# Chunk states in three rounded products, and three changes of order, in a two-layer decoder trunk

## The chip, the cores and the metric

The kernel runs on one core of a Trainium2 chip. A core has a matrix engine (TensorE, PE in the profile; its weight loads are shown apart as PEld), a vector engine (VectorE, DVE), a scalar engine for activations and copies (ScalarE, ACT), a general engine (GpSimd, POOL) and queues that issue transfers (SyncE, SP, and those of the other engines). They run side by side, each through its own list of instructions in order, and wait for each other on semaphores. SBUF is the memory that the engines work in, PSUM holds what PE writes, in banks of 512 numbers a partition.

The metric is the time of one execution on the device in microseconds (us), as the median of several runs.

## What is computed

The reference is a decoder trunk of two layers over 1040 tokens (16 learned ones and 1024 of input) of width 1024, in float32. Layer 0 is a state space mixer, layer 1 attention, and each is followed by a feed forward network (FFN) with a causal convolution.

```python
# mixer, by chunk of tokens
cb = einsum('bclgn,bcsgn->bgcls', c_c, b_c)
y_diag = einsum('bgcls,bgecls,bcsgep->bclgep', cb, decay_in, xdt)
chunk_states = einsum('bclgn,bgecl,bclgep->cbgepn', b_c, decay_to_end, xdt)
state = state * d + s_new            # over the chunks, in order
y_off = einsum('bclgn,cbgepn,bgecl->bclgep', c_c, prev_states, exp(a_cs))
# attention, stick-breaking
logits = einsum('bthd,bshd->bhts', q, k) * scale
log_keep = where(visible, log_sigmoid(-logits), 0)
w = exp(where(visible, log_sigmoid(logits) + later, -inf))
o = einsum('bhts,bshd->bthd', w, v)
# FFN
h = causal_conv(u @ w_up);  g, val = split(h);  (silu(g) * val) @ w_down
```

The mixer has 4 groups of 8 heads, a state of 128 by 64 for each head; attention has 16 heads of width 64.

## The kernel before

**Rounded parts.** A float32 number x is split in a high part, x rounded to the matrix engine's faster format (float32r), and a low part, x less the high one. A product of two such numbers is then made of three products, high by high, high by low and low by high, added in one PSUM bank (`mm3`, lines 209 to 211). Nearly all large products are made so. A high part is a copy on ACT, a low part a subtraction on DVE or POOL.

**The mixer** (`mixer`, `ssd_decays`, `ssd_front`, `ssd_back`). The 1040 tokens lie in nine chunks of 116 (the last has 112). For each of the four groups it runs through the nine chunks; between them it runs pieces of the projections of the next groups (`next(work)`: 24 matmuls with an ACT filter tap and three DVE taps behind them), as many to a chunk as SHARES says: two in groups 0 and, mostly, 3, three or four in groups 1 and 2. In a chunk, `ssd_front` transposes B (`bk`) and x, makes `cbm`, `xdt` (x times dt, on DVE) and `xde` (xdt times the decay to the chunk's end, on POOL in two pieces, behind the pieces of `E` that are made there for the same chunk); then come the projection pieces; then `ssd_back` makes the chunk's state `S` from `bk` and `xde` in one float32 product (line 799), adds it to the running state, and makes the outputs `y`. Eight of the nine chunks of a group have an S: 32 products. The whole loop is written out by hand: PE, DVE, ACT and POOL keep the order of the program (`manual_schedule`).

**Attention** (`attention`, `heads`). Eight pairs of heads, each in 18 steps (i, jj): token block i of 116, key tile jj of 348 tokens, jj from i // 3 down to 0. Steps 0 to 2 have one key tile each, steps 3 to 8 are blocks 3 to 5 with tiles 1 and 0, steps 9 to 17 are blocks 6 to 8 with tiles 2, 1 and 0. A step starts with `weigh`: the logits `lg` on PE (line 1653), two sigmoids on ACT (1654, 1655), two scans and a product `bt` on DVE (1664, 1665). Then come the halves of the projections that fall due (table `halves`, 12 matmuls each), what the step before left in `late`, a chore (rounding the next weights), and `flush`, which transposes the weights of two steps before (`turn`, wT, line 1687) and, when a visit of blocks is done, multiplies the values (`values`, po, line 1710). These four engines keep the program's order here too.

The table `halves` gives the keys so: tile 2 of a pair's own keys at its steps 4 and 5, tiles 0 and 1 of the next pair's keys at steps 8, 9 and 14, 15. For the last pair, tile 2 comes at steps 0 and 1. After the second half DVE multiplies the product by the norm factor (`t`, line 1577); one step later `key` splits `t`: a copy on ACT (line 1588, the high part), a subtraction on DVE (`klo`, line 1589), and three transfers on SP's queue (lines 1590 to 1592) that put the high and low parts of the two heads above each other in the two key tiles. The logits of a head read both halves of its tile. Tile 2 is first read in step 9.

The first half of the output projection runs as units beside the last pair (`o_blocks`): a unit is 12 matmuls into a bank (`accumulate`) and a DVE addition of that bank to `h` (line 538). In the loop of the last pair each step from 5 on runs one unit; after it (`while turns or ready`) two units run ahead of each remaining turn, the first two of them in the two halves of the tile that the logits used.

**FFN, up projection** (`enter_ffn`, `forms`, `up`). The product with w_up is made by a fast scheme of seven half-size products, `product(0)` to `product(6)` of a block, with sums and differences of quarters of the input (`forms`: t1, t2, t3 ... and their rounded parts) and of the weights. The input's second half of tokens is t = 1. A block adds the first sum (`add(y, y, p1)`), and then the third product's sum, `add(z, z, u2)`, line 1237 by its helper, to which product 5 adds. For the first block, `forms` of t = 1 is a generator that advances one `yield` with every part of the block: in its steps it multiplies `h` by the norm's factors (`product(K, ...)` and `product(range(KD // 2, KD), ...)`, eight DVE instructions, line 1091), makes t1 and t2 (line 1115), and rounds the forms (lines 1097, 1098). Here the framework's planner orders the engines by simulated times and the order of the program; `behind` adds a wish for an order that costs no semaphore.

Of the kernel before, what the change touches and what calls it, by code (L numbers as in the profile page):

```python
# [105 lines left out]
class Trunk:  # L106
    def __init__(self, ctx, tc, a):
        self.tc, self.nc, self.a = tc, tc.nc, a
        nc = self.nc
        self.cp = ctx.enter_context(tc.tile_pool(name="cp", bufs=1))  # L110
        self.qp = ctx.enter_context(tc.tile_pool(name="qp", bufs=NQ))
        self.tmps = ctx.enter_context(tc.tile_pool(name="up", bufs=8))
        self.wp = ctx.enter_context(tc.tile_pool(name="wp", bufs=3))
        self.mp = ctx.enter_context(tc.tile_pool(name="mp", bufs=2, space=bass.MemoryType.PSUM))
        self.sp = ctx.enter_context(tc.tile_pool(name="sp", bufs=SMB, space=bass.MemoryType.PSUM))
        self.dp = ctx.enter_context(tc.tile_pool(name="dp", bufs=1, space=bass.MemoryType.DRAM))
        self.lp = None
        self.n = 0
        self.open = []
        self.hold = self.copy_tie = self.silu_tie = None  # L120
        self.consts()
# [406 lines left out]
    def accumulate(self, h, f, s0, n, w, ks, front=0, bank=None, base=0, new=False):  # L528

        ps = (bank or (self.ex if f % 3 == 2 else self.mm))("acc")  # L530
        c, o = slice(s0 - base, s0 - base + n), slice(front + s0, front + s0 + n)
        for i, (hi, lo) in enumerate(ks):
            wh, wl = w(i, f)
            self.mm3(ps[:, :n], wh, wl, hi[:, c], lo[:, c], i == 0, i == len(ks) - 1)
        if new:
            self.nc.vector.tensor_copy(h[f][:, o], ps[:, :n])
        else:
            self.nc.vector.tensor_tensor(h[f][:, o], h[f][:, o], ps[:, :n], op=ALU.add)
# [220 lines left out]
    def ssd_front(self, g, x, bt, ct, c, dk, pool):  # L759
# [16 lines left out]
        if c < 8:  # L776
            bk = pool.tile([P, P], F32, tag="bk", name=self.nm("bk"), bufs=2)
            nc.scalar.activation(bk[:n], pcb[:n, P : 2 * P], AF.Copy)
        cbm = pool.tile([P, CB], F32, tag="cbm", name=self.nm("cbm"), bufs=2)
# [4 lines left out]
        if c < 8:  # L784
            xde = pool.tile([P, GH, 64], F32, tag="xde", name=self.nm("xde"), bufs=2)
            pieces(nc.gpsimd, xde[:n], xdt[:n], self.cols[:n, 2, cc, h0 : h0 + GH].unsqueeze(2).to_broadcast([n, GH, 64]), ALU.mult)
        return xdt, xde, bk

    def ssd_back(self, g, x, c, dk, ce, xdt, xde, bk, states, pool):
# [7 lines left out]
        if c < 8:  # L797
            ps = self.lg("S")
            nc.tensor.matmul(ps, bk[:n], xde[:n].rearrange("p h d -> p (h d)"), start=True, stop=True)  # L799
# [23 lines left out]
    def mixer(self, mx):  # L823
# [12 lines left out]
        with self.tc.tile_pool(name="ssd", bufs=3) as pool:  # L836
# [27 lines left out]
            with self.tc.manual_schedule(engines={E.PE, E.DVE, E.Activation, E.Pool}):  # L864
                ahead = self.ssd_decays(0, rows[0][5], 0, pool)
                dk, ce = next(ahead)
                for g in range(GROUPS):
# [3 lines left out]
                    for c in range(9):  # L871
# [8 lines left out]
                        for _ in range(sum(share[: c + 1]) - given):  # L880
                            next(work)
                            if not begun:
                                begun = True
                                nxt = (g, ct, c + 1) if c < 8 else (g + 1, rows[g + 1][5], 0) if g < 3 else None
                                ahead = self.ssd_decays(*nxt, pool) if nxt else iter([(None, None)])
# [189 lines left out]
    def forms(self, layer, h, r, t, tiles, pool):  # L1075
# [11 lines left out]

        def product(ks, part):
            c = slice(new.start, s.start + N) if part == 0 else slice(s.start + N, new.stop)
            for k in ks:  # L1090
                nc.vector.scalar_tensor_tensor(h[k][:, c], h[k][:, c], self.par(gain, k), r[:, c], op0=ALU.mult, op1=ALU.mult)

# [26 lines left out]
        if t:  # L1119
            product(range(KD // 2, KD), 0)  # L1120
            yield
            product(K, 1)
            yield
            t1 = minus(b12, b11)
            product(range(KD // 2, KD), 1)
            yield
            t2 = minus(b22, t1)
# [73 lines left out]
    def up(self, layer, w0, forms, rest, pool):  # L1201
# [8 lines left out]
        def block(b, t, w, late=None):  # L1210
# [35 lines left out]
            p5 = copy(z)  # L1246
            add(z, z, u2)
            yield
# [266 lines left out]
    def heads(self, u, p, pool):  # L1515
# [4 lines left out]
        class Pair:  # L1520
# [38 lines left out]
            def half(me, kind, j, h, bank=None, parts=2):  # L1559
# [16 lines left out]
                if kind == "k":  # L1576
                    nc.vector.tensor_tensor(t[:, :n], ps[:, :n], u[KD][:, o:e], op=ALU.mult)
                    return [lambda: me.key(j, t)]
                nc.scalar.activation(t[:, :n], ps[:, :n], AF.Copy)
# [139 lines left out]
    def attention(self, u, pool, hd):  # L1719
# [34 lines left out]
        for kind, j, bank in (("k", 0, self.mm), ("q", 0, self.mm), ("k", 1, self.sm), ("q", 1, self.ex)):  # L1754
            for h in range(2):
                for f in first.half(kind, j, h, bank):
                    f()
            if (kind, j) == ("k", 0):
                self.late_factors()
        self.token_factors(u[KD], pool)  # L1760
        for p in range(PAIRS):
            prev = None
            for n, (i, jj) in enumerate(steps):
# [14 lines left out]
                for own, pair in now.items():  # L1778
                    if p + 1 < PAIRS and (own, n) in halves:
                        late += pair.half(*halves[own, n])  # L1780
                for f in todo + chores[:1]:
                    f()
# [7 lines left out]
        banks = iter([lambda s, a=a: both[:, a] for a in range(2)])  # L1790
        self.unit_bank = lambda s: next(banks, self.mm)(s)
        while turns or ready:
            next(behind)
            next(behind)
            flush(0)
        return od, behind
# [261 lines left out]
```

## Time and profile before

| what | before |
|---|---|
| median of 3 runs | 2857.06 us (2851.83 to 2860.83) |
| profiled execution, its own time | 2855.13 us |
| its span, first to last instruction | 2853.3 us |
| granted PE clock, mean | 0.997 |
| ACT, POOL busy | 55%, 55% |
| mixer's chunk loop | about 115 to 600 us |
| attention's steps | about 1538 to 2067 us |
| the up projections' starts | about 830 to 860 and 2157 to 2183 us |

Busy time of an engine is the time in which it ran an instruction; it says nothing of whether that work was on the path that set the end. A row of a group reads: line, engine, operation, what it wrote and read, shapes, count, busy time. A row of the timeline gives start and duration in us, and in brackets the idle time before it with what ended it. "PE x <- DVE y" means that PE stood still until DVE had written y. The granted clock is the share of full speed that the matrix engine was given.

### The profile page before, as it was taken

How to read it: one execution, taken by the hardware profiler on the slowest of the kernel's cores; microseconds unless marked ns; L12 is line 12 of the kernel's file. 1: busy time of each engine (PE TensorE's matmuls, PEld its weight loads, DVE VectorE, ACT ScalarE, POOL GpSimd, SP SyncE). 2: the span in 40 equal slices, each digit the busy share in tenths (PEclk: the TensorE clock that was granted, in tenths of full speed). 3: DMA queues.
4: the chain of work that ended last, by engine and by line, in shares of the span. 5: the costliest groups of instructions: out<-in, count | busy, mean ns of one | idle time of the engine just before them, and what ended most of it. 6: DMA issues, size and time to landing. Idle time of an engine off the chain costs nothing.

```text
span 2853.3 us, 56464 instructions
## 1 busy us (share of the span) xinstructions
PE 2809.2 (98%) x21251; PEld 2691.9 (94%) x21251; DVE 2065.4 (72%) x3936; ACT 1580.2 (55%) x3077; POOL 1578.6 (55%) x2144
## 2 busy tenths in 40 slices
PE   8999999999999999999999999999999999999998
PEld 7989999999999999999999999999899999999888
DVE  5676666668487676767886888888749676766776
ACT  5554554543256555555335777777536555555433
POOL 2366455553519888867763212112254888886881
PEclk9999999999999999999999999999999999999999
DMA  4333333343413222235142222222532222225331
GB/s 119 86 112 93 121 83 125 116 136 101 120 64 96 78 80 78 79 135 176 49 142 77 74 73 69 80 70 57 184 131 77 82 80 82 75 82 185 111 104 67
DMA packets 141740, 281.78 MB, mean 99 GB/s; under 512 B 16307, under 2 KB 71740, under 8 KB 141468
## 3 DMA queue, kind: packets, MB, share of 16 engines
q1 hardware_dynamic: 135844, 267.01, 29.8%
q0 software_dynamic: 2048, 6.49, 0.6%
q10 hardware_dynamic: 3576, 4.67, 0.5%
q8 instruction: 168, 2.75, 0.4%
q14 instruction: 104, 0.85, 0.1%
HBM read 207.79 MB, written 55.42 MB: 92 GB/s over the span
## 4 chain that ended last, share of the span: by engine, by line
PE 91%; DVE 4%; ACT 2%; POOL 1%; issue 1%; DMA 0%; SPq 0%; ACTq 0%; DVEq 0%; POOLq 0%
PE p L209 10%; PE p L210 10%; PE p L211 10%; PE acc L209 8%; PE acc L211 8%; PE acc L210 8%; PE pj L209 8%; PE pj L210 8%; PE pj L211 8%; PE po L1710 3%; PE lg L1653 2%; PE wT L1687 2%; PE y L810 1%; PE S L799 1%; PE y L812 1%; PE ms L1069 1%
## 5 line engine op out<-in xcount | busy, mean ns | idle before, releaser
L102 POOL TENSOR_TENSOR wl<-w,wh 128x256 fp32r<-128x256 f32 x760 | 678.9, 923 | 352.2 <-ACT wh L196 225.4
L209 PE MATMUL pj<-uh,wh 128*128 128x348 f32 (+2 forms) x1536 | 500.4, 326 | 2.1 <-DVE xbc L339 1.4
L210 PE MATMUL pj<-ul,wh 128*128 128x348 f32 (+2 forms) x1536 | 494.9, 322 | 0.8 <-DVE ul L320 0.8
L211 PE MATMUL pj<-uh,wl 128*128 128x348 f32 (+2 forms) x1536 | 492.0, 320 | 0.0
L209 PE MATMUL p<-bh,fh 128*128 128x262 f32 (+1 forms) x1408 | 400.9, 285 | 3.9 <-DVE p L1237 3.7
L211 PE MATMUL p<-bh,fl 128*128 128x262 f32 (+1 forms) x1408 | 401.0, 285 | 0.9 <-POOL fl L102 0.9
L210 PE MATMUL p<-bl,fh 128*128 128x262 f32 (+1 forms) x1408 | 399.2, 284 | 0.0
L102 POOL TENSOR_TENSOR fl<-x,fh 128x256 fp32r<-128x256 f32 x352 | 264.3, 783 | 186.8 <-ACT fh L1174 160.9
L210 PE MATMUL p<-bl,wh 128*128 128x262 f32 (+1 forms) x1040 | 295.6, 284 | 1.1 <-DVE bl L1098 1.1
L209 PE MATMUL p<-bh,wh 128*128 128x262 f32 (+1 forms) x1040 | 295.3, 284 | 0.4 <-ACT ft L1234 0.4
L211 PE MATMUL p<-bh,wl 128*128 128x262 f32 (+1 forms) x1040 | 294.1, 283 | 0.0
L209 PEld LDWEIGHTS pj<-uh,wh 128*128 128x128 f32 x1536 | 288.7, 188 | 4.5 <-ACT xbc L336 1.7
L210 PEld LDWEIGHTS pj<-ul,wh 128*128 128x128 f32 x1536 | 289.2, 188 | 2.4 <-DVE ul L320 1.4
L211 PEld LDWEIGHTS pj<-uh,wl 128*128 128x128 f32 x1536 | 288.7, 188 | 0.1
L339 DVE SCALAR_TENSOR_TENSOR c<-p,params,c 128x260 f32<-128x260 f32 (+1 forms) x528 | 248.4, 480 | 54.7 <-ACT c L336 48.3
L209 PEld LDWEIGHTS p<-bh,fh 128*128 128x128 f32 x1408 | 268.0, 191 | 4.7 <-DVE p L1237 4.1
L211 PEld LDWEIGHTS p<-bh,fl 128*128 128x128 f32 x1408 | 267.1, 190 | 1.6 <-POOL fl L102 1.5
L210 PEld LDWEIGHTS p<-bl,fh 128*128 128x128 f32 x1408 | 267.8, 190 | 0.5 <-DVE bl L1098 0.4
L1234 ACT ACTIVATE ft<-p 128x262 f32<-128x262 f32 (+1 forms) x352 | 133.2, 382 | 179.9 <-DVE p L1237 110.1
L210 PE MATMUL acc<-gl,wh 128*128 128x260 f32 (+1 forms) x672 | 214.2, 320 | 0.0
L211 PE MATMUL acc<-gh,wl 128*128 128x260 f32 (+1 forms) x672 | 213.2, 319 | 0.0
L209 PE MATMUL acc<-gh,wh 128*128 128x260 f32 (+1 forms) x672 | 210.8, 320 | 0.1
(336 smaller groups left out, 7690.6 us busy)
## 6 DMA issues: line engine op xcount, KB each, us to landing
w<-in_w_up SPq DMA_DIRECT2D x88, 512.0 KB
w<-in_w_down SPq DMA_DIRECT2D x44, 512.0 KB
w<-in_w_in SPq DMA_DIRECT2D x40, 512.0 KB
E<-ea_d SPq DMA_DIRECT2D x32, 464.0 KB
D<-acs_d SPq DMA_DIRECT2D x32, 420.5 KB
g<-c SPq DMA_DIRECT2D x88, 130.0 KB
g<-c SPq DMA_DIRECT2D x88, 128.0 KB
b<-g SPq DMA_DIRECT2D x16, 520.0 KB
```

The costliest lines, as they stand in the source:

```text
L102: done.append(eng.tensor_tensor(out[:, c], x[:, c], y[:, c], op=op))
L209: self.behind(mm(out, wh, uh, start=first, stop=False, skip_group_check=joins), tie, "behind the sums of squares")
L210: mm(out, wh, ul, start=False, stop=False, skip_group_check=joins)
L211: self.last_mm = mm(out, wl, uh, start=False, stop=last, skip_group_check=joins)
L339: ins = nc.vector.scalar_tensor_tensor(out, ps[:, o + i : o + i + n], wcol(i), out, op0=ALU.mult, op1=ALU.add)
L799: nc.tensor.matmul(ps, bk[:n], xde[:n].rearrange("p h d -> p (h d)"), start=True, stop=True)
L810: nc.tensor.matmul(y, xdt[:n, i, :], dk[:, i, :], start=True, stop=c == 0)
L812: nc.tensor.matmul(y, state[:, i, :], ce[:, i, :], start=False, stop=True)
L1234: nc.scalar.activation(s[:, :N], ps[:, :N], AF.Copy)
L1653: nc.tensor.matmul(ps[:nt, a, :m], part[:, c0 : c0 + nt], ks[a][:, s0 : s0 + m], start=x == 0, stop=x == 1)
L1687: nc.tensor.transpose(pt[:ns, x * CB : x * CB + nt], bt[:nt, a, x * CB : x * CB + ns], self.ident[:nt, :nt])
L1710: nc.tensor.matmul(po[64 * a : 64 * a + 64, t0:n], v[: CH[c][1], c, 64 * a : 64 * a + 64], wt[a][q][: CH[c][1], r, t0:n], start=x == 0, st ...
```

## The change

There are four edits.

1. The chunk states: `bk` is kept as high and low part (ACT copy, DVE subtraction from PSUM), `xde` is split in high and low part by the new `split_xde` (ACT copy, DVE subtraction), called after the first projection piece of a chunk, and S is made by `mm3`. The tiles `bk`, `xdh`, `xdl` and `xde` have one buffer each.
2. In attention, what a key's second half leaves for the next step is now a function that leaves `key` for the step after that. The first pair's own keys, made ahead of the loop, are split as before.
3. For the first pass of the loop after the last pair, the additions of the two units are collected and run after both units have multiplied.
4. In `forms` for t = 1, the second half of the second factor products moves one `yield` later, in front of t1, and each of them is ordered behind the third sum.

```diff
         if new:
             self.nc.vector.tensor_copy(h[f][:, o], ps[:, :n])
+        elif self.adds is not None:
+            self.adds.append(lambda: self.nc.vector.tensor_tensor(h[f][:, o], h[f][:, o], ps[:, :n], op=ALU.add))
...
-            bk = pool.tile([P, P], F32, tag="bk", name=self.nm("bk"), bufs=2)
-            nc.scalar.activation(bk[:n], pcb[:n, P : 2 * P], AF.Copy)
+            bk = pool.tile([P, 2, P], F32R, tag="bk", name=self.nm("bk"), bufs=1)
+            nc.scalar.activation(bk[:n, 0], pcb[:n, P : 2 * P], AF.Copy)
+            tt(bk[:n, 1], pcb[:n, P : 2 * P], bk[:n, 0].bitcast(F32), op=ALU.subtract)
...
-            xde = pool.tile([P, GH, 64], F32, tag="xde", name=self.nm("xde"), bufs=2)
-            pieces(nc.gpsimd, xde[:n], xdt[:n], self.cols[:n, 2, cc, h0 : h0 + GH].unsqueeze(2).to_broadcast([n, GH, 64]), ALU.mult)
+            xde = [pool.tile([P, GH, 64], dt, tag=t, name=self.nm(t), bufs=1) for t, dt in (("xdh", F32R), ("xdl", F32R), ("xde", F32))]
+            pieces(nc.gpsimd, xde[2][:n], xdt[:n], self.cols[:n, 2, cc, h0 : h0 + GH].unsqueeze(2).to_broadcast([n, GH, 64]), ALU.mult)
         return xdt, xde, bk
+
+    def split_xde(self, xde, c):
+
+        if xde:
+            hi, lo, t = (t[: CH[c][1]] for t in xde)
+            self.nc.scalar.activation(hi, t, AF.Copy)
+            self.nc.vector.tensor_tensor(lo, t, hi.bitcast(F32), op=ALU.subtract)
...
-            nc.tensor.matmul(ps, bk[:n], xde[:n].rearrange("p h d -> p (h d)"), start=True, stop=True)
+            hi, lo = (t[:n].rearrange("p h d -> p (h d)") for t in xde[:2])
+            self.mm3(ps, bk[:n, 0], bk[:n, 1], hi, lo, True, True)
...
                             if not begun:
                                 begun = True
+                                self.split_xde(ops[1], c)
...
-        def product(ks, part):
+        def product(ks, part, tie=None):
...
-                nc.vector.scalar_tensor_tensor(h[k][:, c], h[k][:, c], self.par(gain, k), r[:, c], op0=ALU.mult, op1=ALU.mult)
+                ins = nc.vector.scalar_tensor_tensor(h[k][:, c], h[k][:, c], self.par(gain, k), r[:, c], op0=ALU.mult, op1=ALU.mult)
+                self.behind(ins, tie, "behind the third sum")
...
             product(K, 1)
             yield
+            yield
+            product(range(KD // 2, KD), 1, self.third_sum)
             t1 = minus(b12, b11)
-            product(range(KD // 2, KD), 1)
-            yield
             t2 = minus(b22, t1)
...
-            add(z, z, u2)
+            self.third_sum = add(z, z, u2)
...
-                    return [lambda: me.key(j, t)]
+                    return [lambda: [lambda: me.key(j, t)]]
...
-                for f in todo + chores[:1]:
+                for f in todo:
+                    late += f() or []
+                for f in chores[:1]:
                     f()
...
+        self.adds = []
         while turns or ready:
             next(behind)
             next(behind)
+            for f in self.adds or ():
+                f()
+            self.adds = None
             flush(0)
```

More of the change, by code (lines that the diff above doesn't have):

```diff
@@ L119, in __init__ @@
         self.open = []
-        self.hold = self.copy_tie = self.silu_tie = None
+        self.adds = self.hold = self.copy_tie = self.silu_tie = None
         self.consts()
@@ L1756, in attention @@
                 for f in first.half(kind, j, h, bank):
-                    f()
+                    for g in f() or ():
+                        g()
             if (kind, j) == ("k", 0):
```

## The prediction

> **What bounds the kernel now.** I read the page from the top: busy times, then the chain that ended last, then the waits of the matrix engine (PE).
>
> ```profile
> span 2853.3 us, 56464 instructions
> PE 2809.2 (98%) x21251; PEld 2691.9 (94%) x21251; DVE 2065.4 (72%) x3936; ACT 1580.2 (55%) x3077; POOL 1578.6 (55%) x2144
> PE 91%; DVE 4%; ACT 2%; POOL 1%; issue 1%; DMA 0%; SPq 0%; ACTq 0%; DVEq 0%; POOLq 0%
> ```
>
> PE is busy 98% of the span and makes 91% of the chain. Only two things can move the time: PE work, and PE waits. The profiled execution took 2855.13 us (its span and 1.8 around it), 1.9 below the median of 2857.06; the sums below stand on 2855.13. The waits that this change can touch, in us in total, times, longest:
>
> ```profile
> PE lg L1653 <- ACT bt L1655: 6.3, 11, 0.8
> PE acc L209 <- DVE h L538: 4.3, 2, 3.3
> PE p L209 <- DVE p L1237: 3.7, 2, 1.9
> PE S L799 <- POOL xde L102: 1.4, 3, 0.6
> ```
>
> Each edit has one of these rows or makes one longer. A wait has a second price, seen in stretches of the trace (busy time of PE, PEld, DVE, ACT and POOL; the last three numbers are the granted clock, the DMA share and GB/s):
>
> ```profile
> 844.95:848.35 3.40, 3.40 (x17) 3.40 (x17) 3.40 (x12) 2.97 (x9) 0.00 (x0) 0.50 0.00 0
> 2060.10:2066.90 6.80, 5.87 (x30) 4.74 (x32) 1.30 (x4) 0.00 (x0) 0.00 (x0) 0.50 0.91 329
> 2169.30:2172.70 3.40, 3.01 (x25) 3.02 (x26) 3.40 (x11) 2.71 (x9) 0.00 (x0) 1.00 0.00 0
> ```
>
> After a PE gap of 1.86 us at 841.8 the clock was 0.50 for 3.4 us; after one of 3.31 at 2057.7 it was 0.50 for 6.8; after the other wait of p (3.7 less 1.86, 1.8 us, at 2167.9) it stayed at 1.00. Half clock costs half its length: 1.7, 3.4 and 0 us.
>
> **Chunk states.** 32 products S leave their single form for three rounded ones. First the PE work:
>
> ```profile
> 229.22 0.86 PE S L799 x2
> 1636.69 0.32 PE L210 MATMUL pj<-ul,wh 128*128 128x348 f32 x1
> 1638.29 0.33 PE L211 MATMUL pj<-uh,wl 128*128 128x348 f32 x1
> ```
>
> One S is two records and 0.86 us on the chain. Rounded products of 348 columns start 0.16 apart (ten steps from 1636.69 to 1638.29). The trace has no rounded product of 512 columns: in proportion it is 0.235, three are 0.71 (between 0.48, were the pitch fixed, and 0.86, no gain). I take 0.71, the proportional one: 0.15 x 32 = 5 us less PE work.
>
> Then the new links. S waited for xde (POOL); now it waits for xde, a copy on ACT and a subtraction on DVE. The first two pairs of rows are chunks of groups 3 and 0, the third is of group 1, and the last two rows are the nearest copy and (two pieces) subtractions of this size:
>
> ```profile
> 571.83 1.46 POOL L102 TENSOR_TENSOR xde<-xdt,cols 116x256 f32<-116x256 f32 x2
> 573.34 1.12 PE L799 MATMUL S<-xde,bk 116*128 116x512 f32 x2
> 155.71 1.18 POOL L102 TENSOR_TENSOR xde<-xdt,cols 116x256 f32<-116x256 f32 x2
> 157.42 1.02 PE L799 MATMUL S<-xde,bk 116*128 116x512 f32 x2
> 158.29 1.80 DVE L339 SCALAR_TENSOR_TENSOR xbc<-pj,params,xbc 128x344 f32<-128x344 f32 x3 [2.02 <-ACT xbc L336]
> 235.92 1.18 POOL L102 TENSOR_TENSOR xde<-xdt,cols 116x256 f32<-116x256 f32 x2
> 243.03 0.59 PE L799 MATMUL S<-xde,bk 116*128 116x512 f32 x1
> 855.31 0.62 ACT L1174 ACTIVATE wh<-w 128x512 fp32r<-128x512 f32 x1
> 856.58 1.29 DVE L1178 TENSOR_TENSOR wl<-w,wh 128x512 fp32r<-128x512 f32 x2
> ```
>
> The split takes 0.62 + 0.65 and about 0.05 for each of three hand-overs: 1.4 us. In groups 1 and 2 S starts 6 us after xde: hidden. In groups 0 and 3, 13 chunks have 0.05 (573.29 to 573.34) to 0.9 us. At 157.42 the slack is 0.53, so S would stand 0.9. The chunk behind gets part of that back, because its POOL work starts from DVE work that the late S does not hold (DVE was idle 2.02 us before 158.29, which also hides the extra subtraction of bk, while ACT holds only a tap behind xde). Without that return the 13 waits come to 12, with half of it returned to some 7 to 9; I take 9.5, since the two first chunks, with 0.05, hold their own filters back too. Sum: 9.5 - 5 = **+4.5** (from -10, hidden and at the fixed pitch, to +8).
>
> **Keys a step later.** What it removes: the key's copy stands in ACT's queue between one step's sigmoids and the next and waits for DVE.
>
> ```profile
> 1642.29 0.49 ACT L1588 ACTIVATE k<-k 128x348 fp32r<-128x348 f32 x1 [0.79 <-DVE k L1577]
> 1646.15 0.68 PE L1653 MATMUL lg<-k,qs 128*116 128x232 f32 x4 [0.65 <-ACT bt L1655]
> ```
>
> That is step 11 of pair 1; pairs 0 to 6 show it, seven of the eleven waits, 0.65 each: -4.5. One step later the product that it copies is done, and ACT no longer stands still for it.
>
> What it adds: every key tile moves, also the third of a pair's own keys. Its halves run at steps 4 and 5, its split moved from step 6 to 7, and step 9 is the first whose logits read those columns. Pair 1:
>
> ```profile
> 1630.70 0.88 DVE L1665 TENSOR_TENSOR bt<-bt,kp 116x696 f32<-116x696 f32 x1
> 1631.50 0.51 DVE L1589 TENSOR_TENSOR klo<-k,k 128x344 fp32r<-128x344 f32 x1
> 1633.67 1.64 DVE L1664 TENSOR_TENSOR_SCAN kp<-kp,one 116x349 f32<-116x349 f32 x2
> 1635.42 0.88 DVE L1665 TENSOR_TENSOR bt<-bt,kp 116x696 f32<-116x696 f32 x1
> 1632.62 0.55 SPq L1592 DMA_DIRECT2D k<-klo  x1
> 1633.10:1634.40 1.30, 1.30 (x10) 1.30 (x9) 1.30 (x3) 1.18 (x3) 0.00 (x0) 1.00 0.61 136
> 1635.74 0.60 PE L1653 MATMUL lg<-k,qs 128*116 128x116 f32 x4
> 1700.76 0.88 DVE L1665 TENSOR_TENSOR bt<-bt,kp 116x696 f32<-116x696 f32 x1
> 1700.72 0.49 PE L1653 MATMUL lg<-k,qs 128*116 128x116 f32 x3
> ```
>
> The subtraction (klo) stands behind bt of step 6 and ends at 1632.01. Its two transfers are issued by 1633.17, and the stretch to 1634.40 moves 136 GB/s x 1.3 = 177 KB, both of them (86 KB each): landed 2.39 us after klo's end, 1.3 ahead of the logits of step 9. DVE works without a pause here and is behind PE: bt of step 7 ends at 1636.30, when PE already stands at step 9. The moved klo goes behind that bt. DVE is earlier by the 0.43 that klo leaves in step 6 and later by the same, so klo ends near 1636.3, its transfers land near 1638.7, and the logits wait 1638.7 - 1635.74 = 3.0 us. Pair 2 (last two rows) gives 1701.64 + 2.39 - 1700.72 = 3.3. The pairs follow the one or the other, four of the first and three of the second: 21.9 us. Pair 7 makes these keys at steps 0 and 1 and has time. Of what is queued behind: PE holds that step's projections, which nobody else can start; SP's queue holds the next weights behind the two transfers, and those are wanted steps later. From the other side, transfers that landed on issue would leave 1.7 a pair, and as late as the old slack allows 4.3; I take 3.0 and 3.3, which are measured spans put behind a later start.
>
> Each stall resembles the 3.31 us gap and the 1.86 one; their half clock cost 3.4 and 1.7, that of the third 0. I take 1.7: 7 x 1.7 = 11.9 (0 to 24). Edit: 21.9 - 4.5 + 11.9 = **+29.3**.
>
> The Trainium skill ("TensorE: Matmul & The Clock Gate", Part 1: The HAM clock gate) says that the clock falls to half after an idle window of about 3.4 us, and that the windows run free of the kernel. By that rule a stall of 3.0 to 3.3 never fills a window and the 11.9 is nil. The trace disagrees on the length (1.86 was enough) and agrees that chance has a part (1.8 was not).
>
> **Last units first.** The longest wait of attention's tail:
>
> ```profile
> 2061.03 0.58 PE L209 MATMUL acc<-o,wh 128*128 128x256 f32 x1 [3.31 <-DVE h L538]
> 2060.23 0.74 DVE L538 TENSOR_TENSOR h<-h,acc 128x258 f32<-128x258 f32 x2
> ```
>
> The second unit waits for the first one's add, which DVE reaches only after the last scans. With the adds behind both units no work of DVE stands ahead of it, and what PE does behind it depends on no DVE work later than these two adds. Gone are 3.31 and the 6.8 us of half clock, 3.4: **-6.7** (at least -3.3, were the clock to fall anyway).
>
> **Products behind third sums.** In both FFNs:
>
> ```profile
> 838.64 3.29 DVE L1091 SCALAR_TENSOR_TENSOR h<-h,params,r 128x260 f32<-128x260 f32 x8
> 843.21 0.44 DVE L1237 TENSOR_TENSOR p<-p,ft 128x262 f32<-128x262 f32 x1
> 843.70 0.39 PE L209 MATMUL p<-bh,fh 128*128 128x262 f32 x1 [1.86 <-DVE p L1237]
> 851.07 2.54 DVE L1098 TENSOR_TENSOR bl<-h,bh 128x522 fp32r<-128x522 f32 x4
> ```
>
> The sum at 843.21 moves ahead of four of the eight products and of t1, to about 840.3, and that wait of PE goes. But DVE works from 838.64 to 853.6 without a pause (none of its rows there shows idle time), and PE's later products need the low parts that end it. The order changes, not the amount: PE arrives earlier and waits there. I take **-1** for both (-7, both waits with one half clock, to +3, if the planner's new order is worse).
>
> Sum: 4.5 + 29.3 - 6.7 - 1 = +26.1, so 2881; I say **2880 us**.
>
> **Rivals.**
> - *The stalls come, the half clock does not*: 2881 - 11.9 = 2869. For it: one of three gaps; against: two of three, and these gaps are longer. The skill's rule gives the same.
> - *The keys land in time*, the other side: the stall exists only if klo ends later than 1635.74 - 2.39 = 1633.35. Were DVE ahead there, or the copies issued elsewhere, the edit keeps its -4.5: 2855 + 4.5 - 4.5 - 6.7 - 1 = 2847, faster. Against it: bt of step 7 ends at 1636.30, and the queue is in order.
> - *The split is hidden and the third sums pay*: -5 and -7 in place of +4.5 and -1: 2866. Against: slack of 0.05 in the chunks, DVE's unbroken row.
>
> **Chances.** Forecast 0.60, no half clock 0.20, keys in time 0.12, the third 0.08. The range reaches from 2860 (below it most of the third case's spread and the keys in time, 0.14) to 2893 (above it a second half-clock stretch at most stalls, 0.05). A change below 0.3% (8.6 us) cannot be told from none here. Faster by more: 0.08 (keys in time, two thirds). Within: 0.13 (its rest, and parts of the 2866 and 2869 cases). Slower: 0.79.
>
> **What would show it.** Seven logits waits of about 3 us, 65 us apart, released by a DMA of k or by SP, with 0.50 clock behind most; the waits of logits for ACT down from eleven to four; S waiting for DVE xde parts in groups 0 and 3 and nowhere else; no wait of acc of 3.3; the waits of p moved to DVE bl. I am wrong if the logits of step 9 don't wait, or if S never waits.

## The result

The changed kernel took **2895.72 us**, the median of four runs (2895.36 to 2896.07), against 2857.22 before (four runs). The ratio is 1.0143, with a 95% interval of 1.013 to 1.0156. It is slower, as forecast; 2880 was forecast, and 2893 was the upper end of the range. The profiled execution took 2895.53 us, 40.4 above the one of before.

The head of the page after, and the waits of PE that answer to those of before (us in total, times, longest):

```profile
span 2893.8 us, 56654 instructions
PE 2823.2 (98%) x21283; PEld 2712.7 (94%) x21283; DVE 2118.9 (73%) x4000; ACT 1598.5 (55%) x3109; POOL 1565.5 (54%) x2144
PE 89%; DVE 5%; ACT 2%; DMA 2%; POOL 1%; issue 1%; SPq 0%; ACTq 0%; DVEq 0%; POOLq 0%
```

```profile
PE lg L1666 <- DMA k<-klo: 27.7, 7, 4.3
PE S L209 <- ACT xdh L796: 6.5, 8, 1.8
PE S L210 <- DVE xdl L797: 3.2, 10, 0.8
PE lg L1666 <- ACT bt L1668: 1.9, 4, 0.8
PE acc L209 <- DVE h L540: 1.0, 1, 1.0
PE p L209 <- ACT bh L1110: 1.8, 2, 0.9
PE p L210 <- DVE bl L1111: 1.4, 2, 0.7
PE p L209 <- ACT ft L1247: 2.0, 3, 1.2
```

The first row is new: seven waits of the logits for a transfer of the low part of a key. On the chain, DMA went from 0% to 2%. The waits of the logits for ACT fell from eleven to four, the wait of 3.3 us in the output projection is gone, and the 3.7 us of p for DVE's sum are gone too, with about as much in the last three rows instead.

To see where 40.5 us of span went, I cut the timeline at the first instruction of each stage on PE:

| stage | before, us | after, us | difference | forecast |
|---|---|---|---|---|
| mixer, group 0 | 98.7 | 105.7 | +6.9 | |
| mixer, groups 1 and 2 | 292.7 | 290.1 | -2.7 | |
| mixer, group 3 and what follows to the output projection | 123.1 | 128.9 | +5.8 | |
| mixer, sum | | | +10.1 | +4.5 |
| first up projection, its first 600 products | 82.4 | 83.3 | +1.0 | -0.5 |
| attention, first logits to last | 513.8 | 550.0 | +36.2 | +29.3 |
| from the last logits to the second FFN | 104.0 | 97.7 | -6.3 | -6.7 |
| second up projection, its first 600 products | 81.1 | 81.1 | 0.0 | -0.5 |

The other stages agree within 0.4 us. The +1.0 of the first up projection is this execution's own: it took 81.8 us in e3, e10 and e12 below, which have the same edit, and 81.9 in e8, which leaves the edit out. So each edit did what it was forecast to do, with the sign that was forecast, except the third sums, which did nothing. Two sizes are off: attention by 6.9 us, the mixer by 5.6.

Pair 1 around the new wait (start in us, duration). First SP's queue in the kernel before:

```profile
1628.43 0.48 SPq L1590 DMA_DIRECT2D k<-k  x1
1632.04 0.48 SPq L1591 DMA_DIRECT2D k<-klo  x1
1632.62 0.55 SPq L1592 DMA_DIRECT2D k<-klo  x1
1634.20 0.38 SPq L1534 DMA_DIRECT2D w<-in_w_kv  x1
```

Then the changed kernel: SP's queue, DVE and PE.

```profile
1648.08 0.34 SPq L1547 DMA_DIRECT2D w<-in_w_kv  x1
1648.52 0.38 SPq L1730 DMA_DIRECT2D o_d<-o  x1
1648.99 0.48 SPq L1603 DMA_DIRECT2D k<-k  x1
1651.50 0.48 SPq L1604 DMA_DIRECT2D k<-klo  x1
1652.81 0.46 SPq L1605 DMA_DIRECT2D k<-klo  x1
```

```profile
1646.60 1.46 DVE L1568 SCALAR_TENSOR_TENSOR wl<-w,params,wh 128x128 fp32r<-128x128 f32 x4
1650.16 0.88 DVE L1678 TENSOR_TENSOR bt<-bt,kp 116x696 f32<-116x696 f32 x1
1650.96 0.51 DVE L1602 TENSOR_TENSOR klo<-k,k 128x344 fp32r<-128x344 f32 x1
```

```profile
1655.09 1.00 PE L1666 MATMUL lg<-k,qs 128*116 128x116 f32 x4 [4.03 <-DMA k<-klo]
```

The reader is to see three things. klo stands behind a bt of DVE, as the forecast had it, and ends at 1651.47, 0.4 after the logits could have started (1655.09 less 4.03 is 1651.06). Its second transfer is not issued right behind the first, at about 1652.1, but at 1652.81. And the first copy of the key (line 1603), which in the kernel before went out ahead of the next weights, goes out behind them (512 KB, line 1547) and behind a store of 174 KB. The second low transfer overwrites what that first copy reads, so it has to wait until the copy has landed. The queue's own waits name this: line 1605 waits for the transfer k<-k for 7.0 us in all (in e10 below for 21.4, in e13 not at all).

Why the weights went ahead is seen on DVE. Their load may go out when DVE has read the older weights out of the same buffer, in step 6. Before the change klo stood ahead of that read in the same step (it ended at 1632.01, the read at 1633.32). In the changed kernel klo stands a step behind it: the read ends at 1648.06 (1646.60 and 1.46), and the load is issued at 1648.08.

The clock, in two of the stretches at 0.50 that the change brought (seven in attention, two in the mixer, 3.41 or 6.83 us each; busy time of PE, PEld, DVE, ACT, POOL, then clock, DMA share, GB/s):

```profile
1653.40:1660.00 6.60, 4.92 (x19) 4.89 (x20) 3.61 (x10) 1.96 (x6) 0.81 (x4) 0.50 0.06 13
137.80:141.20 3.40, 3.40 (x34) 3.06 (x32) 3.26 (x11) 1.08 (x2) 0.74 (x2) 0.50 0.45 148
```

### The profile page after: what moved, and what is told of

The parts are those of the page before. It is cut to its first block, busy times and chain, and to the rows that moved or that the text cites. A ratio compares the mean times of both kernels' runs of the same rounds, so it can differ in the third digit from the quotient of the medians.

```text
span 2893.8 us, 56654 instructions
## 1 busy us (share of the span) xinstructions
PE 2823.2 (98%) x21283; PEld 2712.7 (94%) x21283; DVE 2118.9 (73%) x4000; ACT 1598.5 (55%) x3109; POOL 1565.5 (54%) x2144
## 3 DMA queue, kind: packets, MB, share of 16 engines
q1 hardware_dynamic: 135844, 267.01, 29.3%
## 4 chain that ended last, share of the span: by engine, by line
PE 89%; DVE 5%; ACT 2%; DMA 2%; POOL 1%; issue 1%; SPq 0%; ACTq 0%; DVEq 0%; POOLq 0%
PE p L211 10%; PE p L209 10%; PE p L210 10%; PE acc L209 8%; PE acc L211 8%; PE acc L210 8%; PE pj L209 7%; PE pj L210 7%; PE pj L211 7%; PE lg L1666 3%; PE po L1723 3%; PE wT L1700 2%; PE y L821 1%; DMA k<-k 1%; PE ms L1081 1%
## 5 line engine op out<-in xcount | busy, mean ns | idle before, releaser
L1672 POOL TENSOR_SCALAR_AFFINE_SELECT kp<-kp 116x232 f32<-116x232 f32 (+1 forms) x72 | 39.2, 544 | 318.5 <-ACT kp L1667 311.8
```

Of the source, the lines that this page charges most:

```text
L1672: nc.gpsimd.affine_select(out=t[:nt, :, c0 : c0 + nt], in_=t[:nt, :, c0 : c0 + nt], compare_op=ALU.is_gt, fill=fill, base=0, pattern=[[0, ...
```

## The experiments

Unless said otherwise, each is the changed kernel with one edit. Medians are in us; ratios are to the kernel before in the same session, with their 95% intervals.

### 1. Which edit costs what

**The keys split as before (e1).**

```diff
-                    return [lambda: [lambda: me.key(j, t)]]
+                    return [lambda: me.key(j, t)]
```

> The changed kernel with the keys split where they were before (edit 2 undone, all else kept). Theory A (the third key tile's transfers land after the logits of step 9 want them; the seven waits of 27.7 us and the half clock behind them are the loss): attention falls back by the 36.2 us that its stretch grew, 2895.7 - 36.2 = 2859.5 us, no wait of logits for a key transfer, 11 waits of logits for ACT again. Rival B (the loss is in attention's crowded DVE and ACT queues, whatever the key's place): less than half of it comes back, above 2877.

2857.78, ratio 1.0012 (1.0002 to 1.0021). The stretch of attention went from 550.0 back to 512.7 us and the logits again waited eleven times for ACT, 6.3 us. The moved split costs the whole of attention's loss.

**Only the third key tile split as before (e2).**

```diff
-                    return [lambda: [lambda: me.key(j, t)]]
+                    return [(lambda: me.key(j, t)) if j == 2 else lambda: [lambda: me.key(j, t)]]
```

> The changed kernel with only a pair's third key tile split where it was; the two tiles of the next pair stay a step later. Theory A: the stalls go and the gain of the edit (seven waits of 0.65 for ACT, 0.8 with the refill) stays: 2859.5 - 5 = 2854.5 us, four waits of logits for ACT. Rival C (each key that moves costs the same): two of three still move, two thirds of 36.2 stay, 2884.

2855.0, ratio 1.0002 (0.9993 to 1.0011). Attention took 509.9, 2.8 less than in e1 and not 5. The loss sits in the third tile alone. The two other tiles do gain from the later split, but less than the waits for ACT that go: small ones come in their place.

```profile
PE pj L209 <- DVE qs L1618: 1.8, 7, 0.4
```

**The third tile's keys projected two steps earlier, its queries later; all splits stay a step later (e3).**

```diff
-            (0, 0, "v", 1), (0, 2, "q", 2), (0, 4, "k", 2), (0, 6, "v", 2),
+            (0, 0, "v", 1), (0, 2, "k", 2), (0, 4, "q", 2), (0, 6, "v", 2),
```

> The changed kernel with all keys a step later, but the halves of a pair's third key tile at steps 2 and 3 and those of its third query tile at 4 and 5 (before: the other way round). Theory A (it is the deadline of step 9, not the move): split at step 5, transfers land some 6 us ahead of step 9, no stall, about 2855 us. If the queries now land late instead, a wait of logits for qs of under 1 us a pair, 2860. Rival D (a split one step away from its product always puts DVE behind): stalls stay, 2890 or more.

2853.68, ratio 0.9996 (0.9987 to 1.0006); attention 509.4. With two steps more of slack the later split costs nothing.

**The chunk states in one product again (e4).**

```diff
...
-            hi, lo = (t[:n].rearrange("p h d -> p (h d)") for t in xde[:2])
-            self.mm3(ps, bk[:n, 0], bk[:n, 1], hi, lo, True, True)
+            nc.tensor.matmul(ps, bk[:n], xde[:n].rearrange("p h d -> p (h d)"), start=True, stop=True)
...
-                                self.split_xde(ops[1], c)
```

> The changed kernel with the chunk states in one float32 product again (edit 1 undone, all else kept). Theory A (the split's links cost more than the 5.3 us of PE work that it saves, and two half-clock stretches of 3.4 us follow its waits): the mixer falls back by 10.1 us, 2885.6. Rival (only the size of the attention stall is off, and the states cost the 4.5 forecast): 2891.

2887.67, ratio 1.0117 (1.01 to 1.0134): 8.0 below the changed kernel. (The profiled execution, 2884.8, is the shortest of its four and 10.7 below that of the changed kernel.) In it the four groups of the mixer are back at 98.7, 146.3, 146.4 and 123.2 us.

**The third sums as before, on top of e3 (e8).**

```diff
+            t1 = minus(b12, b11)
+            product(range(KD // 2, KD), 1)
             yield
-            product(range(KD // 2, KD), 1, self.third_sum)
-            t1 = minus(b12, b11)
             t2 = minus(b22, t1)
```

> Kernel e3 with the second factor products where they were (edit 4 undone). Theory A (DVE's row is unbroken there, so the order moves PE's wait and not its end): 2853.7 within 2. Rival (the two waits of 1.9 and their half clock were won): 2858 or more.

2853.06, ratio 0.9991 (0.9982 to 1.0), against 2853.68 for e3. The wait is back in full and the time doesn't move:

```profile
PE p L209 <- DVE p L1250: 3.7, 2, 1.9
```

This edit is worth nothing that can be measured, in either direction.

### 2. The half clock, by itself

The wait of the logits can be filled without being shortened. Here 26 products that nothing uses run in front of the logits of step 9 (e5).

```diff
+                if n == 9 and p + 1 < PAIRS:
+                    fill = self.ex("fill")
+                    for _ in range(26):
+                        nc = self.nc
+                        nc.tensor.matmul(fill[:, :348], u[0][0][:, HALO : HALO + P], u[0][0][:, HALO : HALO + 348], start=True, stop=True)
```

> The changed kernel with 26 more matmuls of 348 columns (4.2 us, their result is not used) ahead of the logits of step 9 in pairs 0 to 6: PE works while the key transfers land. It measures what the half clock costs. Theory A: the wait of 4 us stays as long but is no longer idle, so the clock is not halved behind it: attention's stretch was 36.2 longer, of which 28.8 stalls less 6.5 waits removed leave 13.9 for the half clock; 2895.7 - 13.9 = 2882 us, with 0.50 nowhere in attention. Rival (the half clock has nothing to do with the idle time, or costs nothing since DVE is behind anyway): 2895 or, with the matmuls on top, 2925.

2879.84, ratio 1.0085 (1.007 to 1.0101): 15.9 us faster than the changed kernel with 182 products more. The products take the place of the wait:

```profile
1649.03 4.40 PE L1785 MATMUL fill<-uh 128*128 128x348 f32 x26
```

Attention shrank from 550.03 to 536.12, by 13.9, and has no stretch at 0.50 any more, though the products run for 30.5 us in all, where the waits were 27.7. PE's busy time agrees: over attention it was 505.8 us before and 519.5 in the changed kernel, 13.7 more for the same products. So the half clock behind the seven waits costs some 13.9 us, 2.0 a wait. The rest of attention's loss is the waits themselves.

### 3. What sets the length of the wait

**The high part and its transfer at step 6, the low part at step 7 (e9).**

```diff
-                    return [lambda: [lambda: me.key(j, t)]]
+                    return [(lambda: me.key(j, t)) if j == 2 else lambda: [lambda: me.key(j, t)]]
...
+                if j == 2:
+                    return [lambda: me.key_low(j, t)]
+                me.key_low(j, t)
+
+            def key_low(me, j, t):
...
```

> The changed kernel with the high part of the third key tile and its transfer at step 6, as before, and the low part and its two transfers at step 7; the other tiles as in the change. It tells apart why the stall is 4.1 us and not the 3.1 forecast. Theory E (0.6 of it: the first transfer now stands behind 512 KB of weights, and the last one waits for it, since it overwrites what the first one reads): the seven waits fall from 27.7 to about 23.5 us, the last transfer is issued 0.1 us after the one ahead of it. Rival F (all of the extra 1 us is the time from the last byte to the release of PE): 27.7 stays. Time 2895.7 - 4.2 and up to 3 of half clock: 2889 to 2892; with F 2895.

2890.95, ratio 1.0127 (1.011 to 1.0144). The waits of the logits for klo fell from 27.7 to 23.3 in all and attention by 4.7 us, to 545.4. The first copy, sent earlier, no longer holds the last transfer. (In its profiled execution the stage ahead of attention was 4.9 us longer, with a wait of 3.1 in the first FFN that no other kernel here shows, and that has nothing to do with the keys.)

**The split at the start of step 7, ahead of its logits' work on DVE (e10).**

```diff
+                todo, late = late, []
+                if n == 7:
+                    for f in todo:
+                        f()
+                    todo = []
                 bt = self.weigh(i, jj, now[0].qd[i // 3], now[0].ks, prev, pool)
-                todo, late = late, []
```

> The changed kernel with the third key tile split at the start of step 7, ahead of that step's logits, scans and bt, and not behind them: the same step, another place in DVE's queue. Theory A (klo is late because it stands behind the scans and bt of step 7): klo ends 2.5 us earlier, seven waits of 1.1 to 1.7 us (8 to 12 in all, not 27.7), half clock behind few of them: 2861 to 2868. Rival (the step counts, not the place): 2890 or more.

2894.12, ratio 1.0142 (1.0127 to 1.0157). This missed: klo ran earlier, and the waits stayed at 26.9 us. The same rows as above, of this kernel:

```profile
1644.26 1.26 DVE L1568 SCALAR_TENSOR_TENSOR wl<-w,params,wh 128x128 fp32r<-128x128 f32 x4
1645.87 0.50 DVE L1602 TENSOR_TENSOR klo<-k,k 128x344 fp32r<-128x344 f32 x1
```

```profile
1645.55 0.34 SPq L1547 DMA_DIRECT2D w<-in_w_kv  x1
1645.98 0.55 SPq L1730 DMA_DIRECT2D o_d<-o  x1
1646.63 0.48 SPq L1603 DMA_DIRECT2D k<-k  x1
1647.20 0.58 SPq L1604 DMA_DIRECT2D k<-klo  x1
1650.52 0.46 SPq L1605 DMA_DIRECT2D k<-klo  x1
```

```profile
1652.78 1.00 PE L1666 MATMUL lg<-k,qs 128*116 128x116 f32 x4 [3.99 <-DMA k<-klo]
```

klo ends 2.4 us ahead of the point where the logits could start (1648.79), but its last transfer is issued only at 1650.52, 4.15 after it. The weights and the store stand ahead of the first copy, 686 KB. The last transfer waits for that copy. What DVE gained, the queue took.

**e10 with the load of the next key weights ordered behind the key's transfers (e12).** In e10 it goes out at 1645.55, when DVE's last read of older weights has just ended (1644.26 and 1.26, the first of the DVE rows above): it is sent as soon as a buffer is free, far ahead of its use. In e12 the same load, the key weights of pair 3, is issued at 1681.70, behind a key tile made at the end of pair 1, and the loads of that pair's query and value weights follow right behind it (1682.33 and 1682.80). So the one order moves three loads of each pair, and no wait of PE names them.

```diff
-                nc.sync.dma_start(w32, src)
+                ins = nc.sync.dma_start(w32, src)
+                if kind == "k":
+                    self.behind(ins, self.key_sent, "behind the key's transfers")
...
-                nc.sync.dma_start(x[64:, c].bitcast(F32), lo[:64, :n])
+                self.key_sent = nc.sync.dma_start(x[64:, c].bitcast(F32), lo[:64, :n])
```

> The kernel of e10 (the split of the key run ahead of the logits of step 7, which there gave 26.9 us of logits waits all the same) with one order more: on SP's queue the load of a pair's next key weights (512 KB), which the planner had put ahead of the key's three transfers, stands behind the last transfer of the key before it. Nothing else moves. In pair 1 of e10, klo ended at 1646.4, the first copy was issued at 1646.63, behind that load (1645.55) and a store of 174 KB (1645.98), and the transfer that overwrites what the first copy reads was issued only at 1650.52, 4.1 behind klo's end; the logits would have started at about 1648.8 and started at 1652.78. Theory 'the queue': without the load ahead, the last transfer is issued 0.7 behind klo's end and has landed 2.4 behind it, PE is released 0.6 later: the logits wait 0.2 to 1.0 a pair, 2 to 7 in all in place of 26.9, and the half clock in the attention's steps (about 17 us of 0.50 stretches' cost and more in e10) goes: 2853 to 2862. Rival 'one step is too little, whatever the queue': waits stay above 20 and the time at 2889 or more. Between, 2865 to 2885: the bytes of the store still hold the first copy.

2861.3, ratio 1.0021 (1.0011 to 1.003). One change of order on a queue that computes nothing is worth 32.8 us, nearly all of it in attention. That stretch went from 551.0 to 518.1:

```profile
1641.62 0.48 SPq L1605 DMA_DIRECT2D k<-k  x1
1643.52 0.33 SPq L1732 DMA_DIRECT2D o_d<-o  x1
1643.94 0.48 SPq L1606 DMA_DIRECT2D k<-klo  x1
1644.52 0.55 SPq L1607 DMA_DIRECT2D k<-klo  x1
```

```profile
PE lg L1668 <- DMA k<-klo: 6.8, 6, 2.9
```

Here the last transfer follows the one before it by 0.58 and the wait of pair 1 is 0.38. The store still goes ahead in some pairs, in pair 6 with a load of output weights (1967.35), and two waits remain above 1.5 us (1.68 and 2.92, the latter in pair 6), each with a half-clock stretch of 3.41.

**The changed kernel with that same order, the split left where the change put it (e13).** The diff is that of e12, without e10's.

> The changed kernel with the one order of e12 alone: the load of the next key weights behind the key's transfers on SP's queue; the split stays where the change put it. Theory 'two parts: DVE's place sets most, the queue the rest': klo still ends 0.6 behind the nominal start of the logits, its last transfer is issued 0.6 behind klo's end in place of 1.3 and lands 2.4 behind it in place of 3.0, PE starts 0.6 later: a wait of about 3.4 in place of 4.0 in four pairs and 3.6 in place of 4.27 in three, 23.5 to 25 in all in place of 27.7; the half clock stays behind most stalls: 2888 to 2893. If the forecast's 2.39 was right but for the queue alone, waits of 3.0 and 3.3 and 21.9 in all. Rival 'the queue sets all': no waits, 2860 or less. Rival 'the queue sets nothing': 2894 to 2897.

2888.99, ratio 1.0123 (1.0106 to 1.0139), 6.7 below the changed kernel; attention 544.4, which is 5.7 less.

```profile
PE lg L1668 <- DMA k<-klo: 22.5, 7, 3.5
1647.74 0.51 DVE L1604 TENSOR_TENSOR klo<-k,k 128x344 fp32r<-128x344 f32 x1
1648.85 0.55 SPq L1607 DMA_DIRECT2D k<-klo  x1
1651.05 0.59 PE L1668 MATMUL lg<-k,qs 128*116 128x116 f32 x4 [3.20 <-DMA k<-klo]
```

With the queue set free, 5.2 of the 27.7 us of waits go, and the 22.5 that stay come from klo's late place on DVE. The two causes don't simply add: klo early alone (e10) takes 0.8 off, the queue alone (e13) 5.2, both together (e12) 20.9. Both conditions are needed.

### 4. Can it beat the kernel before?

**xde made ahead of E on POOL, on top of e3 (e6).**

```diff
+                taken = 1
...
-                        for _ in ahead:
-                            pass
+                        for _ in range(2 - taken):
+                            next(ahead)
...
+                        for _ in ahead:
+                            pass
...
```

> Kernel e3 (all edits, third key tile ahead of the query tile) with xde made ahead of E in POOL's queue: E's pieces go behind the front of their chunk. Theory A (in groups 0 and 3, S waits because the split starts 0.05 to 0.9 us before PE needs it): xde is 3.5 us earlier, the split is hidden in all groups, the mixer loses its 9.9 us of excess and gains 5.3 of PE work and about 1 of old waits: 2853.7 - 16 = 2837.5 us, waits of S under 1 us. Rival (POOL's row is the loop that paces group 0, and y now waits for E as long): 2847 to 2854, with waits of y for POOL E.

2848.47, ratio 0.9973 (0.9964 to 0.9982), 5.2 below e3, a third of the 16 that were expected. Group 0 went from 104.3 in e3 to 101.6 us and group 3 from 129.1 to 125.4, still above the 98.7 and 123.1 of before. The time is in the rival's range, but the waits for E that it names don't show. The waits of S fell from 9.9 to 4.7, and one wait of y, for D from DVE, rose from 0.9 to 2.0:

```profile
PE S L209 <- ACT xdh L796: 2.6, 3, 1.3
PE S L210 <- DVE xdl L797: 2.1, 5, 0.7
PE y L821 <- DVE D L786: 2.0, 1, 2.0
```

**Three products in groups 1 and 2 only, one float32 product in groups 0 and 3, on top of e3 (e7).**

```diff
...
+            if g in (1, 2):
                 self.mm3(ps, bk[:n, 0], bk[:n, 1], hi, lo, True, True)
+            else:
+                nc.tensor.matmul(ps, bk[:n, 0].bitcast(F32), xde[2][:n].rearrange("p h d -> p (h d)"), start=True, stop=True)
...
-                                self.split_xde(ops[1], c)
+                                self.split_xde(ops[1] if g in (1, 2) else None, c)
```

> Kernel e3 with the three rounded products of S in groups 1 and 2 alone, one float32 product in groups 0 and 3. Theory A: groups 0 and 3 fall back by 6.9 and 5.7 us, groups 1 and 2 keep their 1.33 each: 2853.7 - 12.6 = 2841 us. Rival (the states cost time in some other way than the waits of groups 0 and 3): above 2848.

**2841.15** (2840.6 to 2841.85), ratio 0.995 (0.9936 to 0.9963). This beats both kernels. PE is now 99% busy, and S waits as little as before the change:

```profile
PE 2804.6 (99%) x21267; PEld 2692.4 (95%) x21267; DVE 2087.5 (74%) x3968; ACT 1591.8 (56%) x3093; POOL 1583.6 (56%) x2144
PE S L816 <- POOL xde L102: 1.4, 3, 0.6
```

**e7 with the last units' additions as before (e11).**

```diff
-        self.adds = []
         while turns or ready:
```

> Kernel e7 (edit 1 in groups 1 and 2 only, third key tile ahead of the query tile) with the first two additions after the last pair back between their units (edit 3 undone). Theory A (the second unit waits for the first one's addition, 3.3 us, and half clock follows): 2841.2 + 6.4 = 2847.5 us, a wait of acc for DVE h of 3.3. Rival (the tail gained from something else): 2841.

2846.92, ratio 0.9973 (0.9964 to 0.9983): 5.8 above e7. The stretch from the last logits to the FFN is 102.9 us, against 97.7. The edit of the units holds what it was forecast to bring.

## Why the prediction was right in direction and too low

The sum was +26.1, and the profiled execution came out 40.4 longer. Two terms make up most of what is missing: the keys (29.3 forecast, 36.2 measured), where the step on SP's queue failed, and the chunk states (4.5 and 10.1), where a gain in PE work was counted in two groups that don't get it and the half clock was put at nothing.

**Keys, the waits (21.9 forecast, 27.7 measured).** The mechanism holds: seven waits, in the pairs and at the step named, klo behind the bt of step 7, released by a transfer. The step that failed is the sentence that "SP's queue holds the next weights behind the two transfers". That was the order of the kernel before, and the forecast moved klo without asking what the planner, which orders that queue by when a load's buffer is free, would send in its place. In the changed kernel the weights stand ahead of all three transfers of the key, and the first copy holds the last. "Landed 2.39 us after klo's end", taken from the kernel before with a free queue, became 3.62 from klo's end to PE (1651.47 to 1655.09). With the queue set free (e13) the seven waits are 22.5, against 21.9: the term was right but for the queue. In e13 PE starts 2.8 after klo's end, so 2.39 was 0.4 short of the release; klo itself came 0.2 earlier against the logits than forecast, which makes up for part of it. That 22.5 lies so near to 21.9 is in part luck.

**Keys, the half clock (11.9 forecast, 13.9 measured).** The forecast took the middle of three unlike gaps, 1.7 a wait; e5 gives 2.0. All seven waits had it, not "most". What made the three gaps unlike was not seen: it is in the last section.

The Trainium skill ("TensorE: Matmul & The Clock Gate", Part 1: The HAM clock gate) asks for an idle window of about 3.4 us before the clock falls, and has that window run free of the kernel. By that rule the seven waits of 3.0 to 3.5 us in e13 should mostly have passed; all seven were followed by 0.50, as were all seven of the changed kernel, of e9 and of e10. The lengths of the slow stretches, 3.41 and 6.83, are one and two of the Trainium skill's windows. The traces agree with a window that runs free of the kernel, but 1.86 us of idle time in one was enough.

**Keys, the ACT waits (-4.5 forecast).** The row fell from 6.3 to 1.9, by 4.4. The time gained is smaller, 2.8 (e1 against e2), because projections then wait for DVE's part of the queries. Over attention, the new waits of 27.7, the 13.7 more of PE's busy time, ACT's -4.4 and 0.8 less of a wait for DVE (wT for v, 1.8 to 1.0) make the 36.2 that were measured.

**Chunk states (+4.5 forecast, +10.1 measured).** Groups 0 and 3, before and after (length, then busy time of PE, PEld, DVE, ACT, POOL, clock, DMA share, GB/s):

```profile
114.50:213.22 98.72, 96.22 (x759) 87.92 (x757) 77.42 (x195) 58.75 (x79) 58.87 (x82) 1.00 0.34 102
505.95:629.07 123.12, 122.72 (x934) 114.02 (x933) 78.50 (x190) 62.86 (x99) 77.13 (x106) 1.00 0.38 116
```

```profile
114.11:219.77 105.66, 98.89 (x767) 90.57 (x766) 85.64 (x211) 62.53 (x87) 60.40 (x82) 0.98 0.32 95
509.84:638.76 128.92, 124.89 (x943) 116.37 (x941) 88.23 (x206) 67.48 (x107) 79.75 (x106) 0.99 0.38 111
```

Length less PE's busy time went from 2.50 to 6.77 in the one and from 0.40 to 4.03 in the other. The waits were nearly right: 7.9 more, forecast 9.5. In groups 1 and 2 the gain in PE work was right as well: each S is 0.165 shorter there (0.95 to 0.79 us to the next instruction), 2.7 us for 16. Two things are missing in the forecast. It counted that gain for all 32 products, and in groups 0 and 3, where the three products wait for their parts one after the other, PE's busy time didn't fall: it rose by 2.67 and 2.17. And it priced no half clock behind these waits, though it had done so for the keys; there were two stretches (137.8 and 557.6) of 3.41.

What a stretch costs is seen in executions that lack it. Group 0 took 104.27 us in e3, with PE busy for 97.46, and group 3 took 128.01 in e13, with PE busy for 123.31; so the two stretches cost 1.4 and 0.9 us (one at 125.8 in group 0 of e13 cost 0.1, so the place matters). Without them the waits are 8.6 more than before, PE's work is 1.8 more in groups 0 and 3 and 2.7 less in groups 1 and 2, in sum 7.8; the half clock's 2.3 makes the 10.1. Of the ten traces of kernels with edit 1 as the change has it, four have a stretch in both groups and six in one, and the mixer's loss lies between 7.9 and 10.3 us in them.

**Last units (-6.7 forecast).** Measured -6.3 in the trace and -5.8 in e11 against e7.

**Third sums (-1 forecast).** Nothing (e8). The argument, that DVE works without a pause and PE only waits elsewhere, was right; the 1 us was generous.

**The rivals.** Keys that land in time need klo early and the queue free (e12), or two steps of slack (e3, 2853.68); the change has neither. The half clock came. The chunks' split was not hidden. The range ended too low because its upper end allowed for a second half-clock stretch behind the keys' waits alone, and not for the keys' waits and the chunk states both coming out larger.

## What to carry to other kernels

When work that issues transfers is moved, look at the whole queue that they go through, and ask what else becomes free to go out ahead of them: a load that nobody needs for a long time can stand in front, and an overwrite turns an early copy into a second round trip. A moved split needs slack for its engine, its transfers and their release together, some 3 us here, and both the engine's order and the queue's have to give it. Use a cheaper form of a product only where its added parts have cover, and where PE stands still for some 1.5 us within 3.4 us, in one wait or in several, allow for a second price for the clock.

## What the hardware showed

- **The half clock went by PE's idle time in slices of a fixed grid, and useless work removed it.** In each trace the stretches at 0.50 start on one grid of 3.413 us, to within 0.01: in the changed kernel 137.79, 557.63 and 861.41 lie 123 and 89 steps apart. I counted PE's idle time in the slices of that grid that were at full clock, in all fifteen traces from 60 us to 12 us before the end. All 45 slices with 1.86 us or more were followed by 0.50, and none with less than 0.95; in between (the longest that was not followed had 1.80) some were and some were not, and what decides there stays open. So two waits of nearly the same length in the kernel before could differ. That of 1.86 us lay in one slice, and 0.50 followed. That of 1.83 was cut by a border of the grid, and 1.00 followed. The two slices (length, PE's busy time, and so on as above; the border lies at 2169.3):

```profile
841.50:844.90 3.40, 1.54 (x12) 1.33 (x12) 3.40 (x11) 1.05 (x4) 0.00 (x0) 1.00 0.02 5
2165.90:2169.30 3.40, 1.96 (x17) 1.75 (x15) 3.40 (x11) 0.39 (x1) 0.00 (x0) 1.00 0.00 0
```

  Twenty-eight waits of the logits of 3.0 to 4.3 us in four kernels were all followed by 3.41 or 6.83 us at 0.50. In e12 the waits of 1.68 and 2.92 were followed by it as well, one of 0.95 was not. In group 0 of the changed kernel two waits close together (1.02 and 0.76 us, within 2.3 us) fell in one slice and were followed by the stretch at 137.8; in e3 and e10 a border cut the second of the same two waits, and no stretch followed. Filling the waits saved 13.9 us of attention.
- **A transfer of 86 KB takes about 2.2 us from issue to the engine that waits for it.** From the issue of the last key transfer to the first product: 2.28 (changed kernel), 2.26 (e10), 2.20 (e13), 2.19 (e12). The Trainium skill ("DMA: Bandwidth & Descriptors", Anatomy of one DMA — SWDGE (gpsimd) path) gives about 2.0 us of fixed cost and bytes over 436 GB/s for transfers issued by GpSimd; these were issued by SP, and by that formula 86 KB would take an estimated 2.2. The runs agree.
- **Three rounded products of 512 columns** take 0.165 us less than one float32 product, where nothing waits between them.
